# The first norm of a decoder layer on Trainium2: three blocks ahead, then two groups of three

## The chip, the cores and the metric

One core of a Trainium2 chip runs the whole kernel. The metric is the device time of one execution in microseconds. The engines are TensorE (PE, with its weight loads as PEld), VectorE (DVE), ScalarE (ACT), GpSimd (POOL) and SyncE (SP). Each of PE, DVE, ACT and POOL works through its own list of instructions in order; SP only issues transfers.

## What is computed

One step of a hybrid decoder layer for 1024 prompt tokens and 32 sample tokens (8 sequences of 4), model width 1024. Cut to what matters here:

```
h = rmsnorm(x, norm1)                       # x: 1056 tokens x 1024
z = h @ w_in                                # 6216 columns, split below
hq, hf, hi, hog, aq, ak, av, iq, ik, iw, ga, gb = split(z)
y_a = (rmsnorm(hgrn2(hq, hf, hi)) * silu(hog)) @ w_a     # gated recurrence, 4 heads
y_b = sparse_attention(aq, ak, av, iq, ik, iw) @ w_b     # top-256 keys of an indexer, 4 heads
x = x + (sigmoid(ga) * y_a + sigmoid(gb) * y_b) @ w_o
x = x + square(relu(rmsnorm(x, norm2) @ w_up)) @ w_down
y = rmsnorm(x, norm_f)
```

with `rmsnorm(x, g) = x * rsqrt(mean(x * x) + eps) * g`. The sample tokens also attend to 256 cached tokens of their sequence, whose pages are gathered.

## The kernel before

**First norm.** The 1056 tokens are nine blocks: 0 to 7 of 128 tokens, block 8 of 32. For each block: load `xt`; on ACT a Square with a running sum into `ssx`; `rstd_of` (lines 183 to 193) makes the reciprocal root `rsx` of it, with a variance step on DVE, a Sqrt on ACT, a Reciprocal and three short refinement steps on DVE; one DVE multiply writes the normed `ht` (L234); eight PE transposes turn it into a PSUM tile `hTp` (L238); ACT copies that to `hh`, rounded to fp32r (L239), and DVE takes the rest, `hl = hTp - hh` (L240). The blocks go through in `GROUPS`: 0, 1 and 2 singly, then (3, 4), (5, 6), (7, 8), and a group shares one `rsx`.

**Products.** Each product of `h` with a weight is made of three fp32r products: high by high, low by high, high by low (`gemm3`, lines 152 to 158). A weight tile is loaded into `wr` (one buffer), ACT casts its high part (L148) and DVE subtracts for its low part (L149), in `wload`, both at high priority. The first two weights are `whi` and `whog` of head 0; they are called in the loop when block 2 has been squared. The tokens are cut into three chunks of 352 columns, so chunk 0 needs blocks 0 to 2, chunk 1 blocks 2 to 5. `proj_two` runs chunk by chunk over the two weights, with 24 PE instructions for each weight and chunk.

**PSUM.** Eight banks: two of tag `g` (accumulators of the projections), two of tag `t` (single banks) and two pairs of tag `s`. `hTp` takes a pair of tag `s`, so a block's transposes wait until the copies of the block two before it have been made.

**Behind it.** The raw `xt` blocks are transposed too (`xTp`, L253, with an identity `idr` that is made from the last group's `rsx`), copied by ACT and stored by POOL for the residual. Then come, head by head, the recurrence, then the indexer and its top-k by bisection on DVE and ACT, with the gate projections `wgt` as work for PE beside it, then attention: scores `S`, DVE mask and maximum, ACT exponential (L896), PE transposes `pTp`, copies `pT` by ACT or DVE (L888), products `po`. For the sample group gathered value pages `vpg` are cast by ACT (`vsh`, L970) and split by DVE (`vsl`, L971). Merge, output projection and MLP follow.

**What sets the order.** The program is written in the order of the text, but a list scheduler with a timing model of its own places the instructions on each engine by their dependences and priorities. A change in one place can therefore set other places in another order.

Of the kernel before, what the change touches and what calls it, by code (L numbers as in the profile page):

```python
# [10 lines left out]
F32 = mybir.dt.float32  # L11
# [3 lines left out]
AF = mybir.ActivationFunctionType  # L15
ALU = mybir.AluOpType
# [3 lines left out]
D = 1024  # L20
# [15 lines left out]
N_UNITS = 26  # L36
DOTS_S, DOTS_L = "sstts", "sstsstss"
CUTS = (0, 352, 704, 1056)

GROUPS, FIRST_W = ((0,), (1,), (2,), (3, 4), (5, 6), (7, 8)), 2  # L40

TH, TC = 528, 264
ORDER = ("P1", "P2", "P6", "P5", "P7", "P4", "P3")
# [18 lines left out]
C_HQ, C_HF, C_HI, C_HOG, C_AQ, C_AK, C_AV, C_IQ, C_IK, C_GA, C_GB = (  # L62
    0, 512, 1024, 1536, 2048, 2560, 3072, 3584, 4096, 4168, 5192)
# [37 lines left out]
def hybrid_step(ctx: ExitStack, tc, x_prompt, x_sample, cache_k, cache_v, cache_idx_k, state_hgrn,  # L101
# [3 lines left out]
    nc = tc.nc  # L105
    dbg = dbg or {}

    cst = ctx.enter_context(tc.tile_pool(name="cst", bufs=1))
# [10 lines left out]
    def ps_t(name):  # L119
        return psum.tile([128, 512], F32, name=name, tag="t", bufs=2)  # L120

    def ps_s(name):
        return psum.tile([128, 2, 512], F32, name=name, tag="s", bufs=2)
# [5 lines left out]
    ident = cst.tile([128, 128], F32, name="ident")  # L129
# [8 lines left out]
    hh = big.tile([128, 8, T], F32R, name="hh", tag="hh")  # L138
    hl = big.tile([128, 8, T], F32R, name="hl", tag="hl")


    def wload(rows, c0, nk, m, name):
        raw = wp.tile([128, nk, m], F32, name=name + "r", tag="wr", bufs=1)
        nc.sync.dma_start(raw, rows[:, c0:c0 + m].rearrange("(k p) m -> p k m", p=128))
        wh = wp.tile([128, nk, m], F32R, name=name + "h", tag="wh", bufs=2)
        wl = wp.tile([128, nk, m], F32R, name=name + "l", tag="wl", bufs=2)
        with tc.high_priority():
            nc.scalar.copy(wh, raw)  # L148
            nc.vector.tensor_tensor(wl, raw, wh.bitcast(F32), op=ALU.subtract)  # L149
        return wh, wl  # L150

# [31 lines left out]
    def rstd_of(ss, n, scale, name):  # L183
        rt = sm.tile([128, 3, 9], F32, name=name, tag="rs", bufs=2)
        v, r, t = (rt[:ss.shape[0], a, :n] for a in range(3))
        nc.vector.tensor_scalar(v, ss, scale, EPS, op0=ALU.mult, op1=ALU.add)
        nc.scalar.activation(r, v, AF.Sqrt)
        nc.vector.reciprocal(r, r)

        nc.vector.scalar_tensor_tensor(t, r, -0.5, r, op0=ALU.mult, op1=ALU.mult)  # L190
        nc.vector.tensor_tensor(t, t, v, op=ALU.mult)
        nc.vector.scalar_tensor_tensor(r, t, 1.5, r, op0=ALU.add, op1=ALU.mult)
        return r
# [7 lines left out]
    g1 = U.get([128, 1024], F32, "g1")  # L201
    nc.scalar.dma_start(g1, bass.AP(tensor=norm1.tensor, offset=norm1.offset, ap=[[0, 128], [1, D]]))

    def tok(tb):
        n = 128 if tb < 8 else NS
        return n, slice(tb * 128, tb * 128 + n)
# [3 lines left out]
    nc.scalar.activation(zc, ones[:, 0:1], AF.Sqrt)  # L210
    hr = Ring(U, 6)
    xts = []
    first_w = None
    for grp in GROUPS:
        ss = sm.tile([128, 3], F32, name="ssx", tag="ssx", bufs=3)
        if 8 in grp:
            nc.vector.memset(ss, 1.0)
        hts = []
        for a, tb in enumerate(grp):
            n, cs = tok(tb)  # L220
            xt = U.get([128, 1024], F32, "xt")
            src = x_prompt[0, cs, :] if tb < 8 else x_sample.rearrange("s q d -> (s q) d")
            nc.sync.dma_start(xt[:n], src)
            ht = hr.get([128, 1024], F32, "ht")
            nc.scalar.activation(ht[:n], xt[:n], AF.Square, accum_out=ss[:n, a:a + 1])
            xts.append(xt)
            hts.append(ht)
        if not first_w and grp[-1] >= FIRST_W:
            first_w = [wload(w_in[0], C_HI, 8, 128, "whi"), wload(w_in[0], C_HOG, 8, 128, "whog")]
        rs = rstd_of(ss[:, :len(grp)], len(grp), 1.0 / D, "rsx")  # L230
        for a, tb in enumerate(grp):
            n, cs = tok(tb)
            ht = hts[a]
            nc.vector.scalar_tensor_tensor(ht[:n], xts[tb][:n], rs[:n, a:a + 1], g1[:n], op0=ALU.mult, op1=ALU.mult)  # L234
            pst = ps_s("hTp")
            pv = pst.rearrange("p a (b c) -> p (a b) c", c=128)
            for k in range(8):
                nc.tensor.transpose(pv[:, k, :n], ht[:n, k * 128:(k + 1) * 128], ident[:n, :n])  # L238
            nc.scalar.copy(hh[:, :, cs], pv[:, :, :n])  # L239
            nc.vector.tensor_tensor(hl[:, :, cs], pv[:, :, :n], hh[:, :, cs].bitcast(F32), op=ALU.subtract)  # L240
    U.put(g1)
    hr.close()

# [3 lines left out]
    for tb in range(NTB):  # L247
        n, cs = tok(tb)
        xT = U.get([128, 8, 128], F32, "xT")
        for k0 in (0, 4):  # L250
            pst = ps_t("xTp")
# [141 lines left out]
    for h in range(4):  # L393
        vT = U.get([128, T], F32, "vT")

        def ev_og(ps, sl, c):
            sg_ = sm.tile([128, CH], F32, name="sgo", tag="c352", bufs=2)
            sg_ = sg_[:, :sl.stop - sl.start]
            nc.scalar.activation(sg_, ps, AF.Sigmoid)
            nc.vector.tensor_tensor(sil[:, sl], ps, sg_, op=ALU.mult)  # L400

        def ev_i(ps, sl, c):
# [29 lines left out]
        b = U.get([128, T], F32, "b")  # L432
# [33 lines left out]
        for c in range(1, 8):  # L466
            e = eb[:, c * 128 + 127:c * 128 + 128]
            nc.vector.scalar_tensor_tensor(S[:, c, :], S[:, c - 1, :], e, puv[:, c, :],
                                           op0=ALU.mult, op1=ALU.add)
# [14 lines left out]
        for s in range(8):  # L484
            e = eb[:, NP + 4 * s + 3:NP + 4 * s + 4]
            nc.vector.scalar_tensor_tensor(sn[:, s, :], s0[:, s, :], e, pu2[:, s, :],
                                           op0=ALU.mult, op1=ALU.add)
# [13 lines left out]
        for li, B in enumerate(LEVELS):  # L501
            n = T if B <= 2 else NP
# [22 lines left out]
            ps = ps_t("lev")  # L525
# [699 lines left out]
    raw = {}  # L1225
# [335 lines left out]
```

## Time and profile before

| | us |
|---|---|
| three runs | 1783.34, 1787.66, 1788.07 |
| their median | 1787.66 |
| the profiled execution | 1783.03 |
| its span, first to last instruction | 1781.3 |
| PE busy | 1713.2 (96% of the span) |
| DVE busy | 1229.4 (69%) |
| ACT busy | 877.3 (49%) |

The busy time of PE is the sum of its instructions' rows; where a row's end is modelled it overlaps the next one's start. A row of a timeline gives the start in us from the first instruction, the length, the engine, the line, the operation, what it writes and reads, and how often it is repeated in the row; in brackets stands how long the engine was idle before it and what ended that. The granted clock is the share of TensorE's full speed.

### The profile page before, as it was taken

How to read it: one execution, taken by the hardware profiler on the slowest of the kernel's cores; microseconds unless marked ns; L12 is line 12 of the kernel's file. 1: busy time of each engine (PE TensorE's matmuls, PEld its weight loads, DVE VectorE, ACT ScalarE, POOL GpSimd, SP SyncE). 2: the span in 40 equal slices, each digit the busy share in tenths (PEclk: the TensorE clock that was granted, in tenths of full speed). 3: DMA queues.
4: the chain of work that ended last, by engine and by line, in shares of the span. 5: the costliest groups of instructions: out<-in, count | busy, mean ns of one | idle time of the engine just before them, and what ended most of it. 6: DMA issues, size and time to landing. Idle time of an engine off the chain costs nothing. (4 is left out here: it accounts for less than half of the span.)

```text
span 1781.3 us, 31007 instructions
## 1 busy us (share of the span) xinstructions
PE 1713.2 (96%) x11980; PEld 1650.2 (93%) x11980; DVE 1229.4 (69%) x2776; ACT 877.3 (49%) x1645; POOL 231.9 (13%) x296
## 2 busy tenths in 40 slices
PE   6999999999999999988999999999999999999997
PEld 6999999998999998886899998999999999999987
DVE  7275584745799997974747568867777676666565
ACT  6456465334578843224733445444444555454432
POOL 1100000013000014650200231000000011111100
PEclk9999999999999999999999999999999999999999
DMA  5411111231223233461543341544444857686752
GB/s 168 134 50 49 50 56 49 62 93 37 69 77 96 75 109 114 156 190 58 160 150 109 109 133 51 199 138 145 139 143 140 287 133 213 161 222 157 202 155 98
DMA packets 162132, 219.77 MB, mean 123 GB/s; under 512 B 12032, under 2 KB 117792, under 8 KB 161984
## 3 DMA queue, kind: packets, MB, share of 16 engines
q1 hardware_dynamic: 138048, 150.76, 26.6%
q0 software_dynamic: 16880, 57.85, 12.5%
q10 hardware_dynamic: 7056, 9.18, 1.5%
q8 instruction: 94, 1.54, 0.4%
q14 instruction: 54, 0.44, 0.1%
HBM read 140.31 MB, written 74.60 MB: 121 GB/s over the span
## 5 line engine op out<-in xcount | busy, mean ns | idle before, releaser
L1336 PE MATMUL pua<-h2P,wP 128*128 128x264 f32 x1248 | 198.8, 285 | 1.1 <-ACT uu L1405 0.9
L1336 PEld LDWEIGHTS pua<-h2P,wP 128*128 128x128 f32 x1248 | 170.7, 188 | 2.0 <-ACT uu L1405 1.7
L1336 PE MATMUL pua<-h2a,wP 128*128 128x264 f32 x960 | 161.2, 287 | 6.4 <-ACT uu L1405 3.2
L1405 ACT COPY uu<-pua 128x264 f32<-128x264 f32 x192 | 72.4, 378 | 174.9 <-PE pua L1336 162.8
L1336 PEld LDWEIGHTS pua<-h2a,wP 128*128 128x128 f32 x960 | 134.2, 188 | 11.1 <-ACT uu L1405 5.8
L156 PE MATMUL wgt<-hh,wgth 128*128 128x352 f32 x384 | 126.1, 328 | 0.0
L158 PE MATMUL wgt<-hh,wgtl 128*128 128x352 f32 x384 | 125.3, 326 | 0.0
L157 PE MATMUL wgt<-hl,wgth 128*128 128x352 f32 x384 | 124.6, 325 | 0.0
L1336 PE MATMUL pua<-h2b,wP 128*128 128x264 f32 x672 | 119.9, 285 | 1.0 <-ACT uu L1405 0.9
L1336 PE MATMUL puc<-h2P,wP 128*128 128x264 f32 x720 | 113.8, 285 | 0.0
L1336 PEld LDWEIGHTS pua<-h2b,wP 128*128 128x128 f32 x672 | 97.3, 188 | 1.8 <-ACT uu L1405 1.4
L1336 PEld LDWEIGHTS puc<-h2P,wP 128*128 128x128 f32 x720 | 98.1, 188 | 0.4 <-DVE h2P L1353 0.2
L777 ACT ACTIVATE jkA<-sc,bstg 128x1024 bf16<-128x1024 bf16 (+5 forms) x93 | 87.1, 936 | 21.3 <-DVE bstg L796 6.0
L1303 DVE TENSOR_TENSOR wP<-w1r,wP 128x512 fp32r<-128x512 f32 (+2 forms) x96 | 62.7, 654 | 33.5 <-ACT wP L1302 33.0
L772 DVE TENSOR_SCALAR_CACHE_REDUCE jkD<-sc,bstg 128x768 bf16<-128x768 f32 (+3 forms) x96 | 84.4, 879 | 0.9
L1302 ACT CAST wP<-w1r 128x512 fp32r<-128x512 f32 (+2 forms) x96 | 56.9, 593 | 45.5 <-PE puc L1336 22.1
L1336 PE MATMUL puc<-h2a,wP 128*128 128x264 f32 x384 | 72.7, 288 | 2.9 <-ACT h2a L1352 0.9
L156 PEld LDWEIGHTS wgt<-hh,wgth 128*128 128x128 f32 x384 | 72.2, 188 | 2.0 <-issue 1.0
L157 PEld LDWEIGHTS wgt<-hl,wgth 128*128 128x128 f32 x384 | 72.3, 188 | 1.1 <-issue 0.5
L158 PEld LDWEIGHTS wgt<-hh,wgtl 128*128 128x128 f32 x384 | 72.1, 188 | 1.2 <-issue 0.6
L1392 POOL TENSOR_SCALAR one<-uu 128x1 f32<-128x1 f32 x30 | 7.7, 257 | 492.5 <-ACT uu L1405 492.5
L1409 DVE TENSOR_TENSOR hd<-puc,uu 128x264 f32<-128x264 f32 x64 | 27.6, 431 | 56.7 <-ACT uu L1405 55.9
(792 smaller groups left out, 5143.2 us busy)
## 6 DMA issues: line engine op xcount, KB each, us to landing
hc_d<-hd SPq DMA_DIRECT2D x56, 264.0 KB, 2.6
x_d<-hd POOLq DMA_DIRECT2D x28, 528.0 KB
h2P<-hc_d SPq DMA_DIRECT2D x45, 264.0 KB, 5.1
sg_d<-gst ACTq DMA_DIRECT2D x48, 176.0 KB, 2.2
h2a<-hc_d SPq DMA_DIRECT2D x32, 264.0 KB, 5.5
wgtr<-in_w_in_dram SPq DMA_DIRECT2D x16, 512.0 KB, 4.1
qb<-q_d POOLq DMA_DIRECT2D x16, 512.0 KB
w1r<-in_w_up_dram SPq DMA_DIRECT2D x16, 512.0 KB, 4.1
```

The costliest lines, as they stand in the source:

```text
L156: nc.tensor.matmul(ps, wh, xh, start=(k == 0), stop=False)
L157: nc.tensor.matmul(ps, wh, xl, start=False, stop=False)
L158: nc.tensor.matmul(ps, wl, xh, start=False, stop=(k == n - 1))
L772: nc.vector.tensor_scalar(jkD[:, 0, :L], SC[i], s if isinstance(s, float) else s[:, a:a + 1], 0.0, op0=op, op1=ALU.add, accum_out=out[:, a ...
L777: nc.scalar.activation(jkA[:, 0, :(i + 1) * 128], src(i), AF.Sign, bias=thr[:, a:a + 1], accum_out=cnt[:, a:a + 1])
L1302: nc.scalar.copy(w[:, 0, :n], src)
L1303: nc.vector.tensor_tensor(w[:, 1, :n], src, w[:, 0, :n].bitcast(F32), op=ALU.subtract)
L1336: nc.tensor.matmul(ps, w[:, a, k], x[:, b, sl], start=(q in "P1P2P5" and k == n_ == 0), stop=(k == k1 - k0 - 1 and n_ == 2), skip_group_ch ...
L1392: eng.tensor_scalar(one, src, 1.0, 1.0, op0=ALU.max, op1=ALU.min)
L1405: nc.scalar.copy(uu[c][:, {"P1": u1, "P6": 1, "P7": 2}[q]], ps)
L1409: nc.vector.tensor_tensor(hd[j][1][:, s2], bank(j, "P5", c), uu[c][:, 2], op=ALU.add)
```

## The change

Blocks 0, 1 and 2 go through the norm up to their multiply before any of them is transposed and split (`norm`, `turn`). Block 2 is transposed into two single banks of tag `t` (`hTq`), four transposes each, and copied in halves. Blocks 3 to 8 go in two groups of three. The weights of head 0 are cast at plain priority; `whi` comes behind block 0. Four tiny DVE instructions make constants that depend on a result: `one` (1.0, from the third norm) is the scale of the first copies and of the cast of `whi`, so that they follow it; `inv` (1/1024, from `hh` of a group's first block) is the factor in the next group's variance; `onel` (1.0, from the last norm) is the scale of the first sigmoid.

```
--- before.py
+++ after.py
@@ -37,8 +37,6 @@
 DOTS_S, DOTS_L = "sstts", "sstsstss"
 CUTS = (0, 352, 704, 1056)
 
-GROUPS, FIRST_W = ((0,), (1,), (2,), (3, 4), (5, 6), (7, 8)), 2
-
 TH, TC = 528, 264
 ORDER = ("P1", "P2", "P6", "P5", "P7", "P4", "P3")
 
@@ -139,13 +137,13 @@
     hl = big.tile([128, 8, T], F32R, name="hl", tag="hl")
 
 
-    def wload(rows, c0, nk, m, name):
+    def wload(rows, c0, nk, m, name, late=None):
         raw = wp.tile([128, nk, m], F32, name=name + "r", tag="wr", bufs=1)
         nc.sync.dma_start(raw, rows[:, c0:c0 + m].rearrange("(k p) m -> p k m", p=128))
         wh = wp.tile([128, nk, m], F32R, name=name + "h", tag="wh", bufs=2)
         wl = wp.tile([128, nk, m], F32R, name=name + "l", tag="wl", bufs=2)
-        with tc.high_priority():
-            nc.scalar.copy(wh, raw)
+        with tc.high_priority() if late is None else ExitStack():
+            nc.scalar.activation(wh, raw, AF.Copy, scale=1.0 if late is None else late)
             nc.vector.tensor_tensor(wl, raw, wh.bitcast(F32), op=ALU.subtract)
         return wh, wl
 
@@ -210,8 +208,9 @@
     nc.scalar.activation(zc, ones[:, 0:1], AF.Sqrt)
     hr = Ring(U, 6)
     xts = []
-    first_w = None
-    for grp in GROUPS:
+
+    def norm(grp, inv=1.0 / D):
+
         ss = sm.tile([128, 3], F32, name="ssx", tag="ssx", bufs=3)
         if 8 in grp:
             nc.vector.memset(ss, 1.0)
@@ -225,19 +224,54 @@
             nc.scalar.activation(ht[:n], xt[:n], AF.Square, accum_out=ss[:n, a:a + 1])
             xts.append(xt)
             hts.append(ht)
-        if not first_w and grp[-1] >= FIRST_W:
-            first_w = [wload(w_in[0], C_HI, 8, 128, "whi"), wload(w_in[0], C_HOG, 8, 128, "whog")]
-        rs = rstd_of(ss[:, :len(grp)], len(grp), 1.0 / D, "rsx")
+        rs = rstd_of(ss[:, :len(grp)], len(grp), inv, "rsx")
         for a, tb in enumerate(grp):
             n, cs = tok(tb)
-            ht = hts[a]
-            nc.vector.scalar_tensor_tensor(ht[:n], xts[tb][:n], rs[:n, a:a + 1], g1[:n], op0=ALU.mult, op1=ALU.mult)
-            pst = ps_s("hTp")
-            pv = pst.rearrange("p a (b c) -> p (a b) c", c=128)
-            for k in range(8):
-                nc.tensor.transpose(pv[:, k, :n], ht[:n, k * 128:(k + 1) * 128], ident[:n, :n])
-            nc.scalar.copy(hh[:, :, cs], pv[:, :, :n])
-            nc.vector.tensor_tensor(hl[:, :, cs], pv[:, :, :n], hh[:, :, cs].bitcast(F32), op=ALU.subtract)
+            nc.vector.scalar_tensor_tensor(hts[a][:n], xts[tb][:n], rs[:n, a:a + 1], g1[:n], op0=ALU.mult,
+                                           op1=ALU.mult)
+        return grp, hts, rs
+
+    def turn(grp, hts, rs):
+
+        for ht, tb in zip(hts, grp):
+            n, cs = tok(tb)
+            if tb == 2:
+
+                pvs = [(k0, ps_t("hTq").rearrange("p (b c) -> p b c", c=128)) for k0 in (0, 4)]
+            else:
+                pvs = [(0, ps_s("hTp").rearrange("p a (b c) -> p (a b) c", c=128))]
+            for k0, pv in pvs:
+                nk = 8 // len(pvs)
+                for k in range(nk):
+                    nc.tensor.transpose(pv[:, k, :n], ht[:n, (k0 + k) * 128:(k0 + k + 1) * 128], ident[:n, :n])
+            for k0, pv in pvs:
+                ks = slice(k0, k0 + 8 // len(pvs))
+                nc.scalar.activation(hh[:, ks, cs], pv[:, :, :n], AF.Copy, scale=one[:, 0:1] if tb < 2 else 1.0)
+                nc.vector.tensor_tensor(hl[:, ks, cs], pv[:, :, :n], hh[:, ks, cs].bitcast(F32), op=ALU.subtract)
+
+
+    normed = [norm((tb,)) for tb in range(3)]
+
+    one = cst.tile([128, 1], F32, name="one")
+    nc.vector.tensor_scalar(one, normed[2][2][:, 0:1], 1.0, 1.0, op0=ALU.max, op1=ALU.min)
+    turn(*normed[0])
+    first_w = [wload(w_in[0], C_HI, 8, 128, "whi", late=one)]
+    turn(*normed[1])
+    turn(*normed[2])
+    inv = 1.0 / D
+    for grp in ((3, 4, 5), (6, 7, 8)):
+        normed = norm(grp, inv)
+        if len(first_w) == 1:
+            first_w.append(wload(w_in[0], C_HOG, 8, 128, "whog", late=1.0))
+        turn(*normed)
+
+        inv = cst.tile([128, 1], F32, name=f"inv{grp[0]}")
+        nc.vector.tensor_scalar(inv, hh[:, 7, tok(grp[0])[1]][:, 127:128].bitcast(F32), 1.0 / D, 1.0 / D,
+                                op0=ALU.max, op1=ALU.min)
+    rs = normed[2]
+
+    onel = cst.tile([128, 1], F32, name="onel")
+    nc.vector.tensor_scalar(onel, rs[:, 0:1], 1.0, 1.0, op0=ALU.max, op1=ALU.min)
     U.put(g1)
     hr.close()
 
@@ -396,7 +430,7 @@
         def ev_og(ps, sl, c):
             sg_ = sm.tile([128, CH], F32, name="sgo", tag="c352", bufs=2)
             sg_ = sg_[:, :sl.stop - sl.start]
-            nc.scalar.activation(sg_, ps, AF.Sigmoid)
+            nc.scalar.activation(sg_, ps, AF.Sigmoid, scale=onel if h == c == 0 else 1.0)
             nc.vector.tensor_tensor(sil[:, sl], ps, sg_, op=ALU.mult)
 
         def ev_i(ps, sl, c):
```

On ACT at the start, from the square root of the second norm (`rsx`; `ht,ssx` is a square, `whih` and `whogh` are the weights' casts), before:

```order
L187 ACTIVATE rsx<-rsx 128x1
L225 ACTIVATE ht,ssx<-xt 128x1024
L239 CAST hh<-hTp 128x8x128
L148 CAST whih<-whir 128x1024
L187 ACTIVATE rsx<-rsx 128x1
L225 ACTIVATE ht,ssx<-xt 128x1024
L239 CAST hh<-hTp 128x8x128
L225 ACTIVATE ht,ssx<-xt 128x1024 x3
L187 ACTIVATE rsx<-rsx 128x2 x2
L225 ACTIVATE ht,ssx<-xt 128x1024
L239 CAST hh<-hTp 128x8x128
L225 ACTIVATE ht,ssx<-xt 32x1024
```

and now:

```order
L185 ACTIVATE rsx<-rsx 128x1
L224 ACTIVATE ht,ssx<-xt 128x1024
L185 ACTIVATE rsx<-rsx 128x1
L224 ACTIVATE ht,ssx<-xt 128x1024 x2
L249 ACTIVATE hh<-hTp,one 128x8x128
L146 ACTIVATE whih<-whir,one 128x1024
L249 ACTIVATE hh<-hTp,one 128x8x128
L224 ACTIVATE ht,ssx<-xt 128x1024
L249 ACTIVATE hh<-hTq 128x4x128 x2
L224 ACTIVATE ht,ssx<-xt 128x1024 x2
L224 ACTIVATE ht,ssx<-xt 32x1024
L185 ACTIVATE rsx<-rsx 128x3
```

The third norm's root has moved ahead of the first copies, two squares stand before the first `hh`, and three squares before the root that blocks 3 to 5 share.

On DVE, from the weight difference `whogl` to the last group's multiplies (`ht`; `rsx` is a root's steps), before:

```order
L149 TENSOR_TENSOR whogl<-whogr,whogh 128x1024
L240 TENSOR_TENSOR hl<-hTp,hh 128x8x128
L188 RECIPROCAL rsx<-rsx 128x2
L240 TENSOR_TENSOR hl<-hTp,hh 128x8x128
L190 SCALAR_TENSOR_TENSOR rsx<-rsx 128x2
L191 TENSOR_TENSOR rsx<-rsx 128x2
L192 SCALAR_TENSOR_TENSOR rsx<-rsx 128x2
L234 SCALAR_TENSOR_TENSOR ht<-xt,rsx,g_88 128x1024
L234 SCALAR_TENSOR_TENSOR ht<-xt,rsx,g_88 32x1024
```

and now:

```order
L147 TENSOR_TENSOR whogl<-whogr,whogh 128x1024
L230 SCALAR_TENSOR_TENSOR ht<-xt,rsx,g_88 128x1024 x3
L250 TENSOR_TENSOR hl<-hTp,hh 128x8x128
L269 TENSOR_SCALAR inv_237<-hh 128x1
L250 TENSOR_TENSOR hl<-hTp,hh 128x8x128
L184 TENSOR_SCALAR rsx<-ssx,inv_237 128x3
L250 TENSOR_TENSOR hl<-hTp,hh 128x8x128
L186 RECIPROCAL rsx<-rsx 128x3
L188 SCALAR_TENSOR_TENSOR rsx<-rsx 128x3
L189 TENSOR_TENSOR rsx<-rsx 128x3
L190 SCALAR_TENSOR_TENSOR rsx<-rsx 128x3
L230 SCALAR_TENSOR_TENSOR ht<-xt,rsx,g_88 128x1024 x2
```

The last group's reciprocal stood between two `hl`; now the multiplies of blocks 3 to 5 come first, then their three `hl`, and the reciprocal of blocks 6 to 8 behind these.

On PE at the same place, the end of chunk 0 of `whog` up to chunk 1 of `whi`, before:

```order
L157 MATMUL whog<-hl,whogh 128x352
L158 MATMUL whog<-hh,whogl 128x352
L253 MATMUL xTp<-idr,xt 128x128 x8
L238 MATMUL hTp<-ident,ht 128x128 x8
L253 MATMUL xTp<-idr,xt 128x128 x4
L156 MATMUL whi<-hh,whih 128x352
L157 MATMUL whi<-hl,whih 128x352
L158 MATMUL whi<-hh,whil 128x352
```

and now:

```order
L246 MATMUL hTp<-ident,ht 128x128 x16
L156 MATMUL whog<-hh,whogl 128x352
L154 MATMUL whog<-hh,whogh 128x352
L155 MATMUL whog<-hl,whogh 128x352
L156 MATMUL whog<-hh,whogl 128x352
L154 MATMUL whog<-hh,whogh 128x352
L155 MATMUL whog<-hl,whogh 128x352
L156 MATMUL whog<-hh,whogl 128x352
L246 MATMUL hTp<-ident,ht 128x128 x24
L287 MATMUL xTp<-idr,xt 128x128 x8
L246 MATMUL hTp<-ident,ht 128x32 x8
L287 MATMUL xTp<-idr,xt 128x128 x4
```

Before, the transposes of blocks 3 to 7 are spread over chunk 0, the last eight of them standing among `xTp`; now those of blocks 3 and 4 stand behind 17 products of `whog` (with all 24 of `whi` ahead of them) and those of 5, 6 and 7 in one row behind its end, with block 8 before chunk 1.

On ACT in the attention stage, from the last copy `pT` ahead of the first `vsh` to the second, before (`gst` is a gate's copy, `s__` with a number an exponential):

```order
L888 COPY pT<-pTp 128x512
L896 ACTIVATE s__7451,mx<-s__7451,mx 128x256
L970 CAST vsh<-vpg 128x1024
L357 COPY gst<-wgt 128x352
L358 DMA sg_d<-gst 128x352
L148 CAST wgth<-wgtr 128x1024
L357 COPY gst<-wgt 128x352
L358 DMA sg_d<-gst 128x352
L896 ACTIVATE s__7469,mx<-s__7469,mx 128x384
L970 CAST vsh<-vpg 128x1024
L357 COPY gst<-wgt 128x352
L888 COPY pT<-pTp 128x128
```

and now:

```order
L922 COPY pT<-pTp 128x512
L1004 CAST vsh<-vpg 128x1024
L930 ACTIVATE s__7454,mx<-s__7454,mx 128x256
L391 COPY gst<-wgt 128x352
L392 DMA sg_d<-gst 128x352
L930 ACTIVATE s__7472,mx<-s__7472,mx 128x384
L922 COPY pT<-pTp 128x128
L922 COPY pT<-pTp 128x256
L930 ACTIVATE s__7492,mx<-s__7492,mx 128x512
L922 COPY pT<-pTp 128x384
L1004 CAST vsh<-vpg 128x1024
L930 ACTIVATE s__7515,mx<-s__7515,mx 128x640
```

The second `vsh` has moved from ahead of the 128-wide `pT` to behind the 384-wide one.

## Rows read from the trace of the kernel before

**Rows 1.** Waits of PE, whole run: us in total, times, longest us.

```profile
PE hTp L238 <- DVE rsx L186: 14.5, 3, 9.8
...
PE po L891 <- ACT pT L888: 9.0, 6, 6.0
```

**Rows 2.** Windows of 50 us: window, length, busy us (and instructions) of each engine.

```profile
50.00:100.00 50.00, 50.00 (x331) 49.40 (x330) 21.20 (x28) 26.59 (x41) 5.30 (x6) 1.00 0.37 107
```

**Rows 3.** Timeline of PE at the start.

```profile
21.33 1.94 PE L238 MATMUL hTp<-ident,ht 128*128 128x128 f32 x8 [1.03 <-DVE ht L234]
...
22.92 0.64 PE L156 MATMUL whi<-hh,whih 128*128 128x352 f32 x1
...
25.76 0.32 PE L158 MATMUL whi<-hh,whil 128*128 128x352 f32 x1
...
25.92 0.32 PE L156 MATMUL whi<-hh,whih 128*128 128x352 f32 x1
...
35.56 1.04 PE L238 MATMUL hTp<-ident,ht 128*128 128x128 f32 x8
...
36.79 0.40 PE L156 MATMUL whi<-hh,whih 128*128 128x352 f32 x1
...
39.20 0.68 PE L238 MATMUL hTp<-ident,ht 32*128 32x32 f32 x8
```

**Rows 4.** Timeline of ACT at the start.

```profile
11.77 1.01 ACT L239 CAST hh<-hTp 128x1024 fp32r<-128x1024 f32 x1 [0.79 <-PE hTp L238]
...
12.68 1.05 ACT L148 CAST whih<-whir 128x1024 fp32r<-128x1024 f32 x1
...
16.71 1.05 ACT L225 ACTIVATE ht<-xt 128x1024 f32<-128x1024 f32 x1
```

**Rows 5.** Timeline of DVE at the start.

```profile
11.96 0.15 DVE L186 TENSOR_SCALAR rsx<-ssx 128x1 f32<-128x1 f32 x1
...
15.09 0.15 DVE L188 RECIPROCAL rsx<-rsx 128x1 f32<-128x1 f32 x1
...
15.27 0.16 DVE L190 SCALAR_TENSOR_TENSOR rsx<-rsx 128x1 f32<-128x1 f32 x1
...
16.94 1.28 DVE L234 SCALAR_TENSOR_TENSOR ht<-xt,rsx,g 128x1024 f32<-128x1024 f32 x1
...
27.09 1.22 DVE L240 TENSOR_TENSOR hl<-hTp,hh 128x1024 fp32r<-128x1024 f32 x1
...
32.56 0.29 DVE L246 TENSOR_SCALAR idr<-ident,zc 128x128 f32<-128x128 f32 x1
...
34.17 0.79 DVE L311 TENSOR_SCALAR scr<-scr 128x64 int32<-128x64 int32 x7
```

**Rows 6.** Loads of block 4 (issue; landing after it) and of `whog`.

```profile
5.94 0.62 SPq L223 DMA_DIRECT2D xt<-in_x_prompt_dram  x1
...
xt<-in_x_prompt_dram SPq DMA_DIRECT2D x1, 512.0 KB, 7.9
...
whogr<-in_w_in_dram SPq DMA_DIRECT2D x1, 512.0 KB, 5.5
```

**Rows 7.** A window behind the wait at 800 (PEclk third from the end), and slow products.

```profile
804.00:811.00 7.00, 4.32 (x14) 3.15 (x15) 3.90 (x11) 3.75 (x8) 1.98 (x2) 0.52 0.30 90
...
150.18 0.49 PE L156 MATMUL whf<-hh,whfh 128*128 128x352 f32 x1
...
150.47 0.49 PE L157 MATMUL whf<-hl,whfh 128*128 128x352 f32 x1
```

**Rows 8.** Timelines of PE and ACT around 806 us.

```profile
806.22 0.79 PE L891 MATMUL po<-pT,vt 128*128 128x128 f32 x2 [6.00 <-ACT pT L888]
...
804.60 1.04 ACT L970 CAST vsh<-vpg 128x1024 fp32r<-128x1024 f32 x1 [6.66 <-DMA vpg<-in_cache_v_dram,ids]
...
805.89 0.27 ACT L888 COPY pT<-pTp 128x128 f32<-128x128 f32 x1
...
809.80 0.48 ACT L888 COPY pT<-pTp 128x384 f32<-128x384 f32 x1 [0.76 <-PE pTp L885]
```

## The prediction

> **What bounds the kernel now.** First read the list of waits of TensorE (PE) over the whole run: 14.5 us stand before `hTp`, the transposes of the first norm, and 9.0 us before `po` in the attention stage, 6.0 of them in one piece [rows 1]. Then the windows: from 50 to 100 us PE is busy all the time [rows 2]. What the change does at the start therefore reaches the end whole, unless a later stage has slack to swallow it. So the start is followed instruction by instruction in the timelines of PE, ScalarE (ACT) and VectorE (DVE) [rows 3 to 5], and compared at one mark: the first product of chunk 1 of `whi`, at 36.79 us before [rows 3]. By then PE has done `hTp` of blocks 0 to 7, twelve `xTp`, and chunk 0 of `whi` and `whog`. In the changed order block 8 is turned ahead of that mark too, which takes 0.68 us before [rows 3]; so the mark to beat is 37.47.
>
> **The change, step by step.** The clock times below come from walking the changed rows with the durations of before: on ACT a square 1.05 us, a full copy 0.91 to the next start [rows 4], half copies 0.5, an estimate, since they read half as much; on DVE a difference `hl` or `wl` 1.22, a multiply 1.28, each of the four short steps from reciprocal to multiply 0.18 to 0.2 [rows 5].
>
> *Third norm, earlier.* The variance of block 2 is ready at 11.96 + 0.15 [rows 5]. Its square root follows at once, at 12.15, where it stood behind two copies that run until 13.6 [rows 4]. Reciprocal 12.4, multiply 13.15 to 14.45, against 16.94 before [rows 5]; its transposes into the two extra banks take 1.94 us [rows 3], to 16.4.
>
> *First copies, later.* The squares of blocks 3 and 4 now stand ahead of the first `hh`. Block 4 lands at 5.94 + 7.9 = 13.84 [rows 6], so its square starts at 13.85 and `hh` of block 0 at 14.9, where it ran at 11.77 [rows 4]. `whih` 15.8, `hh` of block 1 16.7, the square of block 5 17.6, the half copies 18.7 and 19.2. DVE follows: `hl` of block 0 15.9, `whil` 17.1, `hl` of block 1 18.3, the first half of `hl` of block 2 done at 20.3. Dense work on `whi` chunk 0 begins at 20.4, against 22.92 for its first product [rows 3]. That is the change's gain, some 2.5 us, as long as PE can go on.
>
> *Second group, later.* Blocks 3 to 5 share one square root, which stands behind the squares of 6, 7 and 8 (19.7, 20.75, 21.8): 22.85. `whogh` 22.95, `whogl` 24.0 to 25.2. The load of `whog` is issued when `whil` is done, 18.3, and lands 5.5 later by its old duration [rows 6], at 23.8; that would move these two by 0.85, which is hidden, since PE comes to them later still. Multiplies from 25.2, the last ready at 29.1.
>
> *What PE then does.* It has 24 products of `whi` and 17 of `whog` in its queue ahead of the first transpose of block 3. A product starts 0.16 us after the last one from 25.76 on [rows 3]; at half clock, later in the run, 0.29 [rows 7]. Taking the slow one until 25.65, where before's turned quick, 18 are done by then and 23 more take 3.7 us: block 3 starts at 29.35. Bounds: if all run quickly, the last 15 wait for `whogl` at 25.2 and end at 27.7; if none does, 32.5.
>
> *The chain behind it.* Eight quick transposes take 1.04 us [rows 3]. Block 3 is turned at 30.4, its `hh` done 31.4, its `hl` 32.65: only now is its bank free for block 5, 32.7 to 33.75. `hh` of 5 34.8, `hl` of 5 36.0. In DVE's order the reciprocal of blocks 6 to 8 stands behind this `hl`; four short steps and the multiply end at 38.05. PE, which has nothing ready between, stands from 33.7 to 38.1: 4.4 us. Block 6 to 39.15; block 7 behind its own multiply to 40.45. `idr` stands behind the last multiply (40.6) and seven short operations of 0.11 (seven took 0.79) and takes 0.29 [rows 5]: 41.65, another 1.2 us of waiting, then eight `xTp` to 42.75. Block 8 needs the bank of block 6, whose `hl` stands behind `idr` and seven more short ones, 42.45 to 43.65: 1 us again. Block 8 to 44.35, four `xTp`, and the mark at 44.85. Each row overlaps the next by 0.05 to 0.1 us, so over this chain the sum is some 0.4 too long: 44.45.
>
> Sum of the start: 44.45 - 37.47 = **+7.0 us**; with the bounds of block 3's start, +5.3 to +10.1.
>
> *Edits at nothing.* `one`, `inv` and `onel` are four DVE instructions on one column, of the 0.15 us of the variance row [rows 5], counted where they stand in the chain. Copies that scale, in place of plain ones: the trace has none of this form; between nothing and 0.1 us for each of ten, most of it under waits; I take none. SyncE issues its loads in the same order; `whog` alone comes later, above, and the two loads behind it are not wanted before chunk 2. GpSimd's `xT_d` stores follow `xT` by the same shift, and nobody waits for them. From about 75 to 480 us the orders of all engines are as before, so the shift goes through.
>
> *The attention stage.* From the top-k to about 830 us the scheduler also sets another order; behind it the order is as before. The one place that rows price is the 6.00 us wait [rows 8]: the second `vsh` cast, waiting for its gather until 804.60, stands ahead of the `pT` copy that `po` needs. Now it stands behind the 384-wide `pT`. From the start of the 128-wide one to the end of that it was 809.80 + 0.48 - 805.89 = 4.4 us [rows 8]. But the 39 gate products (6.2 us at 0.16) that stood between the last `po` and the first transpose of this head are now spent earlier, so the gather, issued when `vsl` is done, comes that much later against PE. Bounds: 6.0 gained, where the gather has landed when the cast is reached; 6.2 - 4.4 = 1.8 lost, where the cast holds the next exponential instead. The rest of the permuted rows I price at nothing, between 3 us lost and gained, half of that one wait. I take 0 for the stage, nearer to the loss, because PE's filler is worth its own time wherever it stands.
>
> So 1783.03 + 7.0 + 0 = 1790.0 against the profiled execution. That one lies with the fastest of the three runs (1783.34), 4.6 below their median of 1787.66; against the median it is 1787.66 + 7.0 = **1794.7**.
>
> **A clock that falls in the new waits.** In the wait that ended at 806.22 [rows 8] the granted clock fell: it is 0.52 from 804 to 811, the lower of its two levels of 1.2 and 2.4 GHz [rows 7]. The wait of 4.4 us from 33.7 is shorter, but transposes with two more waits follow it. If the clock falls there, blocks 6 and 7 take 1.94 each, the eight `xTp` as much, block 8 and four more some 2.2: the mark comes 1.5 later, and the start costs +8.5. The Trainium skill, "TensorE: Matmul & The Clock Gate", Part 1, says that the clock drops to 1.2 GHz when the engine idles and comes back after sustained matmul work. By that rule the fall is to be expected, and the sum would be +8.5 and not +7.0; the wait at 800 agrees with it.
>
> **Rivals.**
> 1. *Forecast*: the start loses 7.0, the stage gives nothing: 1794.7. For it: every step is an in-order queue whose rows are known. 0.52.
> 2. *The clock falls in the waits of 33 to 44 us*, or chunk 0 runs slowly to its end: 1787.66 + 8.5 to 10.1 = 1796 to 1798. For it the fall after 800; against it the shorter wait. 0.14.
> 3. *Not slower, because the wait at 800 goes*: the gather lands before the cast is reached. That takes 6.0 us and the low clock behind it, about 1.5: 1787.66 + 7.0 - 6.0 to 7.5 = 1787 to 1789. It decides as soon as the gather lands within 4.4 us of the first `pT`. Against it the moved gate products. 0.26, of which 0.03 with further gains there, below the line.
> 4. *The early start holds*: PE does not stand at block 6 and keeps its 2.5 us: 1785. It would need `hl` of block 5 to be no longer ahead of the reciprocal, which the order denies, or a far quicker copy. 0.08, of which 0.03 with the gain of rival 3.
>
> **How the numbers follow.** A measurement of this kernel can tell about 0.3%, 5.4 us, from no change: the line on the slow side is 1793. Of the forecast 0.36 lie above it and 0.16 below (the start near its lower bound, or some gain in the stage). Slower: 0.36 + 0.14 = 0.50. Same: 0.16 + 0.23 + 0.05 = 0.44. Faster: 0.03 + 0.03 = 0.06. The range runs from rival 4 at 1785, which takes in rival 3, to 1801: the upper bound of the start, 10.1, with the stage's 3 lost.
>
> **What would show it.** After: dense `whi` from about 20 us, block 3 turned near 29, a PE wait of 3 to 5 us before block 6 that ends with its multiply on DVE, two of about 1 us behind it, chunk 1 of `whi` at 43 to 46; from there to 480 us the same work 6 to 9 us later. In the attention stage either the wait of `po` on `pT` is down from 9.0 to about 3, or a wait of several us stands a few blocks later. The forecast is wrong if chunk 1 starts before 41, or if PE's waiting from 650 to 900 us differs by more than 4 us from before.

## The result and the profile after

The changed kernel takes 1799.21 us (median of 15 runs, 1792.39 to 1805.33) beside 1787.06 us of the kernel before (15 runs): ratio 1.0065, 95% interval 1.005 to 1.008, so 9 to 14 us slower, 11.6 by the ratio. Beside the experiments on another chip it came out at 1.0076 (1.005 to 1.0101). The forecast, 1794.7, had the sign and stands in its range, but the loss is larger than its 7.0: of its two terms the start came out at 7.0 and 8.4 us in two profiled executions, and the attention stage, taken at nothing, costs 5 to 7 us.

From the page of the changed kernel: its span, PE's busy time and PE's clock in 40 slices.

```profile
span 1798.4 us, 31000 instructions
...
PE 1723.3 (96%) x11980; PEld 1658.5 (92%) x11980; DVE 1228.6 (68%) x2776; ACT 879.7 (49%) x1645; POOL 231.4 (13%) x296
...
PEclk8999999899999999999999999999999999999999
```

The waits of PE over the whole run (us in total, times, longest), as in [rows 1]:

```profile
PE S L904 <- DVE mx L908: 5.9, 4, 3.5
PE po L925 <- DVE pT L922: 5.4, 3, 3.7
...
PE hTp L246 <- DVE ht L230: 4.8, 2, 4.5
PE whi L154 <- ACT hh L249: 4.8, 1, 4.8
PE po L925 <- ACT pT L922: 3.3, 6, 0.9
```

The 9.0 us of `po` behind ACT's `pT` are down to 3.3, as rival 3 wanted; two waits of 3.5 and 3.7 us, for DVE, stand in their place. At the start 4.8 us stand before `whi` and 4.5 before block 6.

The start on PE, as in [rows 3]:

```profile
14.50 1.09 PE L246 MATMUL hTq<-ident,ht 128*128 128x128 f32 x8 [0.80 <-DVE ht L230]
20.35 0.66 PE L154 MATMUL whi<-hh,whih 128*128 128x352 f32 x1 [4.76 <-ACT hh L249]
...
30.17 1.91 PE L246 MATMUL hTp<-ident,ht 128*128 128x128 f32 x16
...
39.13 3.65 PE L246 MATMUL hTp<-ident,ht 128*128 128x128 f32 x16 [4.46 <-DVE ht L230]
...
45.85 0.41 PE L154 MATMUL whi<-hh,whih 128*128 128x352 f32 x1
```

One row of ACT's timeline, the square of block 3:

```profile
13.36 1.06 ACT L224 ACTIVATE ht<-xt 128x1024 f32<-128x1024 f32 x1 [1.01 <-DMA xt<-in_x_prompt_dram]
```

Two windows (busy us of PE, weight loads, DVE, ACT and GpSimd; the granted clock is third from the end):

```profile
37.10:43.90 6.80, 4.77 (x23) 4.80 (x24) 6.69 (x22) 2.76 (x4) 1.13 (x2) 0.50 0.00 0
...
50.00:100.00 50.00, 50.00 (x334) 49.18 (x333) 13.89 (x23) 24.23 (x39) 7.97 (x9) 1.00 0.43 130
```

The mark, the first product of chunk 1 of `whi`, is at 45.85, 8.4 behind 37.47; from 50 to 100 us PE has no slack, as in [rows 2]. The row of ACT tells where a part of the 8.4 is from: the square of block 3 waits 1.01 us for its load. In the other profiled execution of the same kernel (e9 below) that square found its load there. Its ACT:

```profile
12.16 0.20 ACT L185 ACTIVATE rsx<-rsx 128x1 f32<-128x1 f32 x1 [1.15 <-DVE rsx L184]
12.49 1.06 ACT L224 ACTIVATE ht<-xt 128x1024 f32<-128x1024 f32 x1
...
14.78 1.10 ACT L249 ACTIVATE hh<-hTp,one 128x1024 fp32r<-128x1024 f32 x1
```

and its PE:

```profile
19.49 0.66 PE L154 MATMUL whi<-hh,whih 128*128 128x352 f32 x1 [3.01 <-ACT hh L249]
...
28.81 1.91 PE L246 MATMUL hTp<-ident,ht 128*128 128x128 f32 x16
...
37.78 3.65 PE L246 MATMUL hTp<-ident,ht 128*128 128x128 f32 x16 [4.46 <-DVE ht L230]
...
44.50 0.41 PE L154 MATMUL whi<-hh,whih 128*128 128x352 f32 x1
```

and a window of it:

```profile
35.10:41.90 6.80, 4.12 (x20) 4.15 (x21) 6.66 (x24) 2.13 (x2) 0.60 (x2) 0.50 0.00 0
```

Here the mark is 7.0 late, 1.35 earlier than in the first execution. Of that, 0.86 stands at the first product of `whi` (19.49 against 20.35) and goes with the load. The other 0.5 stands in chunk 0, where 16 products ran at the lower clock here (starts 0.29 apart) and 20 in the first execution. The chain that the forecast walked stands on DVE in the first execution: the difference of block 5, then the reciprocal of blocks 6 to 8, the short steps, the multiplies.

```profile
35.76 1.23 DVE L250 TENSOR_TENSOR hl<-hTp,hh 128x1024 fp32r<-128x1024 f32 x1 [0.91 <-ACT hh L249]
36.90 0.17 DVE L186 RECIPROCAL rsx<-rsx 128x3 f32<-128x3 f32 x1
...
37.70 2.48 DVE L230 SCALAR_TENSOR_TENSOR ht<-xt,rsx,g 128x1024 f32<-128x1024 f32 x2
```

**The attention stage.** Two executions of one kernel can lie 12 us apart by 480 us (last section), so spans don't tell what a stage costs. A window that begins and ends at the same products does: from 600 us of before to 845, 1380 products. Of the kernel before:

```profile
600.00:845.00 245.00, 225.09 (x1380) 202.69 (x1379) 191.89 (x462) 95.42 (x194) 85.17 (x65) 0.99 0.39 121
```

of the changed kernel:

```profile
612.30:862.00 249.70, 228.27 (x1380) 205.37 (x1379) 192.52 (x480) 100.96 (x203) 85.06 (x65) 0.97 0.38 118
```

and of its other execution:

```profile
608.30:860.00 251.70, 231.14 (x1380) 207.38 (x1379) 192.51 (x480) 100.80 (x203) 85.13 (x65) 0.96 0.38 117
```

The stage is 4.7 and 6.7 us longer in the changed kernel. PE's idle time is nearly the same: 245.0 - 225.1 = 19.9 before, 21.4 and 20.6 after. What grew is the busy time of the same 1380 products, by 3.2 and 6.0 us, and the granted clock fell from 0.99 to 0.97 and 0.96. Two long waits stand in it. PE's timeline of the changed kernel, with the short wait ahead of the first:

```profile
679.35 0.71 PE L925 MATMUL po<-pT,vt 128*128 128x128 f32 x4 [0.46 <-ACT pT L922]
683.52 2.50 PE L904 MATMUL S<-kT,qT 128*128 128x512 f32 x4 [3.46 <-DVE mx L908]
...
818.37 1.77 PE L925 MATMUL po<-pT,vt 128*128 128x128 f32 x8 [3.68 <-DVE pT L922]
```

DVE's at the first of them, and the window behind it:

```profile
681.48 0.25 DVE L873 TENSOR_SCALAR pm<-jkD 128x384 bf16<-128x384 bf16 x1
...
682.90 0.56 DVE L908 CUSTOM_DVE_ANT_0 s__6497<-S,pm 128x384 f32<-128x384 f32 x1
```

```profile
682.20:689.00 6.80, 5.13 (x13) 3.80 (x14) 6.80 (x16) 1.51 (x4) 0.00 (x0) 0.50 0.00 0
```

The two other windows of the stage at the lower clock, the first of them behind the second wait:

```profile
818.70:822.10 3.40, 3.15 (x12) 1.86 (x11) 1.21 (x6) 0.61 (x2) 2.49 (x4) 0.50 0.50 152
839.20:842.60 3.40, 3.40 (x17) 3.06 (x16) 1.11 (x3) 2.52 (x4) 0.00 (x0) 0.50 0.00 0
```

The scores `S` of a row block wait until DVE has read an earlier block's scores out, which needs the mask `pm` of the top-k selection. In the kernel before, `pm` was written at 665.03 and the same `S` stood at 667.08, with other products of PE ahead of it and no wait (DVE's row, then PE's):

```profile
665.03 0.26 DVE L839 TENSOR_SCALAR pm<-jkD 128x384 bf16<-128x384 bf16 x1
...
667.08 1.35 PE L870 MATMUL S<-kT,qT 128*128 128x512 f32 x4
```

Counted from the start of its window, PE was ready for this `S` at nearly the same place (67.1 us before, 67.8 in the changed kernel), but DVE wrote `pm` at 65.0 before and at 69.2 now: in the new order it is DVE that comes later.

In the kernel before, the clock fell within the one wait of 6.0 us [rows 8] and stayed at the lower level for 6.8 us by the trace's clock records, from 803.9 to 810.7 [rows 7]. In the changed kernel 13.7 us of the stage are at that level: 6.8 from within the wait of 3.5, 3.4 behind the wait of 3.7, and 3.4 at 839.2, where no wait ahead is longer than 0.8. In the other execution it is 20.5: 6.8 and 13.7, at two waits of 3.4. The Trainium skill, "TensorE: Matmul & The Clock Gate", section "HAM oscillation — how this bites in real kernels", prices such a time at half of itself; the trace agrees: 13.7 - 6.8 = 6.9, half 3.4, where busy time grew 3.2, and 20.5 - 6.8 = 13.7, half 6.9, where it grew 6.0.

### The profile page after: what moved, and what is told of

It is laid out like the page before. It is cut to its first block, busy times and chain, and to the rows that moved or that the text cites. A ratio compares the mean times of both kernels' runs of the same rounds, so it can differ in the third digit from the quotient of the medians.

```text
span 1798.4 us, 31000 instructions
## 1 busy us (share of the span) xinstructions
PE 1723.3 (96%) x11980; PEld 1658.5 (92%) x11980; DVE 1228.6 (68%) x2776; ACT 879.7 (49%) x1645; POOL 231.4 (13%) x296
```

## The experiments

Ratio and interval are against the kernel before on the same chip; its medians were 1790.9 (e1 to e4), 1782.7 (e5 to e8) and 1781.3 (e9 to e12). "Start" is the delay of the mark (against 37.47, or 36.79 where block 8 still stands behind it, as before); for e4 and e11 it is that of the mark and the time of the added transposes behind it. "Stage" is the length of the 1380 products less 245.0. Both are from the one profiled execution; the time in us is worked out from the ratio.

| | start | stage | sum | ratio (interval) | us |
|---|---|---|---|---|---|
| changed kernel | +8.4 | +4.7 | 13.1 | 1.0065 (1.0050 to 1.0080) | +11.6 |
| e9, the same again | +7.0 | +6.7 | 13.7 | 1.0076 (1.0050 to 1.0101) | +13.5 |
| e10, stage order back | +7.4 | 0.0 | 7.4 | 1.0023 (1.0005 to 1.0042) | +4.1 |
| e2, block 5 banks | +6.7 | +0.7 | 7.4 | 1.0027 (1.0009 to 1.0046) | +4.8 |
| e3, free root | +4.7 | +5.3 | 10.0 | 1.0048 (1.0029 to 1.0066) | +8.6 |
| e5, both | +3.2 | 0.0 | 3.2 | 1.0009 (0.9995 to 1.0022) | +1.6 |
| e6, norms only | +1.8 | +0.3 | 2.1 | 1.0024 (1.0010 to 1.0038) | +4.3 |
| e7, filled wait | +8.5 | -0.6 | 7.9 | 1.0032 (1.0019 to 1.0045) | +5.7 |
| e8, banks only | +2.1 | -0.2 | 1.9 | 0.9986 (0.9970 to 1.0002) | -2.5 |
| e12, as e8 | +1.7 | +0.4 | 2.1 | 1.0008 (0.9990 to 1.0025) | +1.4 |
| e4, shift | +4.3 | +1.2 | 5.5 | 1.0003 (0.9984 to 1.0023) | +0.5 |
| e11, stage order alone | +1.1 | +3.8 | 4.9 | 1.0015 (0.9998 to 1.0031) | +2.7 |
| e1, control | +0.5 | -0.5 | 0.0 | 0.9999 (0.9975 to 1.0022) | -0.2 |

**e1, control.** No edit.

> The kernel before, unchanged, run as if it were a change: its ratio to itself should be 1.000 within 0.002. It gives the granted clock of its single runs, which the comparison of the change lacks. Theory A (the start costs some 8 us, and the permuted attention stage the other 4 of the 12 us between the medians): its mean granted clock lies where the changed kernel's does in its quicker runs, 0.987 to 0.991. Theory B (the start costs some 8, and the other 4 are stretches at the lower clock, which come more often with the changed kernel): it stays at 0.990 to 0.993 in nearly all runs, where the changed kernel shows 0.983 to 0.991.

Its mean granted clocks are 0.985 to 0.992 in 12 runs, so theory B's "0.990 to 0.993 in nearly all" fell, and A's words on the clock fit. What the lower clock has to do with the stage came out only with the window of equal products.

**e2, block 5 banks.**

```
-            if tb == 2:
+            if tb in (2, 5):
```

> The changed kernel with block 5 also transposed into two single banks of its own. The start stays as it is but for 0.4 us (block 5 need not wait for the bank of block 3), and the scheduler's order of the attention stage falls back to that of the kernel before. Mark (first product of chunk 1 of whi) at 45 to 46 by both theories. Theory A (the permuted attention stage costs 4 us): 1787 + 8 = 1795, and from 660 to 830 us the delay against before stays at that of the mark. Theory B (the order of that stage is worth nothing, the rest is low clock, met anywhere): 1797 to 1800, as the changed kernel.

The mark at 44.21 is 0.8 ahead of what both theories expected, 45 to 46 (they started from 45.85, the execution with the late load). The stage, +0.7, is as theory A says; the time, +4.8, is below its +8, which the interval just holds. B's +10 and more is outside.

**e3, free root.**

```
-    inv = 1.0 / D
...
-        normed = norm(grp, inv)
+        normed = norm(grp)
...
-        inv = cst.tile([128, 1], F32, name=f"inv{grp[0]}")
-        nc.vector.tensor_scalar(inv, hh[:, 7, tok(grp[0])[1]][:, 127:128].bitcast(F32), 1.0 / D, 1.0 / D,
-                                op0=ALU.max, op1=ALU.min)
```

> The changed kernel with 1/D a constant, so that the square root of blocks 6 to 8 need not wait for hh of block 3. On DVE the multiplies of 6 to 8 then stand right behind those of 3 to 5, ahead of the three hl, not behind them. If the 4.5 us wait before block 6 comes from the root and the reciprocal standing behind hh and hl of blocks 3 to 5, as the prediction's chain has it: that wait goes, block 5 waits for hl of block 3 instead (about 1.5 to 2 us more), idr is there by 36, the mark comes at 40 to 42, and the time is 1787 + 3 to 5 = 1790 to 1792 if the attention stage, whose order is a third one here, gives nothing. If the groups of three are the cause by themselves (one chain of three multiplies, two banks for three blocks), the wait only moves: mark at 44 to 46, 1795 to 1799.

The start's chain is confirmed (rows of DVE, then of PE): the multiplies of 6 to 8 follow those of 3 to 5, ahead of the three `hl`; block 5 now waits 2.63 us for the bank of block 3, and block 6, turned right behind it, no longer 4.46 for its own multiply; the mark is at 41.48, in the range of the first theory. The time is not (+8.6): the stage, which stands in a third order here, is 5.3 longer as well.

```profile
26.38 3.67 DVE L230 SCALAR_TENSOR_TENSOR ht<-xt,rsx,g 128x1024 f32<-128x1024 f32 x3
...
30.76 3.67 DVE L230 SCALAR_TENSOR_TENSOR ht<-xt,rsx,g 128x1024 f32<-128x1024 f32 x3
```

```profile
35.74 3.10 PE L246 MATMUL hTp<-ident,ht 128*128 128x128 f32 x16 [2.63 <-DVE hl L250]
...
41.48 0.41 PE L154 MATMUL whi<-hh,whih 128*128 128x352 f32 x1
```

**e4, shift.** In the kernel before, ahead of the transposes of block 8:

```
+            for k in range(56 if tb == 8 else 0):
+                nc.tensor.transpose(pv[:, k % 8, :n], ht[:n, (k % 8) * 128:(k % 8 + 1) * 128], ident[:n, :n])
```

> The kernel before, with 56 more transposes of 0.13 us into the bank of block 8 ahead of its own: 7.3 us of work on PE at the start and no new wait; every engine's order is otherwise that of before but for four chunk-boundary swaps. If a delay at the start reaches the end whole and nothing else comes with it: 1787 + 6.5 to 7.3 = 1793.5 to 1794.5, and the granted clock as in the control. If a mere shift of the later stages brings low-clock stretches or new waits of its own: 1798 to 1800. If a later stage swallows it: under 1791.

The edit was smaller than meant: block 8 has 32 rows, a transpose of it takes 0.066 us, and the 56 took 3.67. Of that +0.5 (-2.9 to +4.1) was found: it neither shows nor excludes that 3.7 us reach the end whole.

**e5, both.** The edits of e2 and e3 together.

> Both edits at once: the root of blocks 6 to 8 free (1/D a constant), and block 5 in two banks of its own; with the second the attention stage stands in the order of the kernel before again. If the permuted attention stage costs some 5 us (A), this is the free root's start (mark 41.5, 4.7 later than in the kernel before) with that stage's price gone: 4 to 5 us over the kernel before, about 1.0025, and from 640 to 850 us no delay is added. If the order of that stage is worth nothing and the excess is low clock met by chance (B): 1.0045 to 1.005, as with the free root alone.

Start +3.2, stage 0.0, time +1.6. The interval, -0.9 to +3.9, leaves out B's 1.0045 by far and A's +4 to 5 by little: A's stage is as expected, its start and its time came out smaller. It is 7 us less than e3, which differs by the banks of block 5 and the stage's order; start and stage of the two profiles differ by 1.5 and 5.3, together 6.8.

**e6, norms only.**

```
-    first_w = [wload(w_in[0], C_HI, 8, 128, "whi", late=one)]
+    first_w = [wload(w_in[0], C_HI, 8, 128, "whi")]
```

and the same for `whog`, plain scales for the first `hh`, and the free root of e3.

> The changed kernel without its bindings: the casts of whi and whog ranked first as before, the first copies hh not held behind the third norm, the last root free. What is left of the change is three norms written ahead, the two banks for block 3 of the tokens and the groups of three; the attention stage stands in the order of before. If the late start comes from the bindings (copies held behind the squares, the root held behind hh): the mark within 2 us of before's 36.8 and 0.999 to 1.0015. If groups of three cost by themselves (three multiplies in a row on DVE ahead of the first hl): the mark 3 to 5 later and 1.002 to 1.003. If the early norms bring their 2.5 us once nothing holds the rest: 0.9985 and the first dense product at 20 to 21.

The mark is at 39.25: 2.5 behind 36.8, past the 2 of the first theory and short of the 3 of the second, and 1.8 late when block 8, which is turned ahead of it here, is counted. The ratio is above the first theory's range and in that of the second. So the two can't be told apart here. The early gain of the third is excluded: the third norm falls behind the first cast again, and block 2 is transposed at 18.44, as before.

**e7, filled wait.** 28 more transposes, of the rows of block 5, ahead of those of block 6 (the lines that set `fill` are left out).

```
+            if tb in fill:
+                src, m = fill[tb]
+                for k in range(m):
+                    nc.tensor.transpose(pvs[0][1][:, k % 8, :n], src[:n, (k % 8) * 128:(k % 8 + 1) * 128], ident[:n, :n])
```

> The changed kernel with 28 more transposes (of the rows of block 5, into the bank of block 6, which block 6 then overwrites) in the wait of 4.5 us before block 6; 3.6 us of work at full clock, so the wait falls to about 1. The attention stage stands in the order of before. If the clock falls because of that wait (rival 2): the granted clock stays at its upper level from 37 to 44, blocks 6 and 7 take 2 us instead of 3.65, and from the first product of whi to the mark it is 24.0 us, where it was 25.5; the time 1.001 to 1.003. If the fall has another cause: 25.5 again.

PE's rows, then the window that was at 0.50:

```profile
33.76 3.28 PE L246 MATMUL hTp<-ident,ht 128*128 128x128 f32 x28
38.03 1.09 PE L250 MATMUL hTp<-ident,ht 128*128 128x128 f32 x8 [0.99 <-DVE ht L230]
...
43.27 0.65 PE L250 MATMUL hTp<-ident,ht 32*128 32x32 f32 x8 [2.89 <-DVE inv L278]
...
45.95 0.64 PE L154 MATMUL whi<-hh,whih 128*128 128x352 f32 x1
```

```profile
35.00:42.00 7.00, 4.19 (x35) 3.51 (x33) 6.86 (x20) 2.59 (x3) 1.13 (x2) 1.00 0.00 0
```

Filling the wait keeps the clock up from 35 to 42 us, as rival 2 says; but the mark does not move: 45.95 - 20.47 = 25.5 from the first product of `whi`, as in the changed kernel's first execution. Two differences cancel in that number: chunk 0 ran quicker here, 8.7 us up to block 3 against 9.8, and from block 3 to the mark it took 16.8 against 15.7 in both executions of the changed kernel. Blocks 6 and 7 are turned faster, block 8 then waits 2.89 us for DVE, and the clock falls behind that wait, at 44.8 by the clock records. The order near block 8 differs a little, so this shows that DVE can set the mark, not what the fall costs there.

**e8 and e12, banks only.** In the kernel before, block 2 in two banks, its copies in halves.

> The kernel before with one part of the change alone: block 2 transposed into two single banks, its copies in halves; nothing else, and the attention stage as before. No bank was waited for there in the kernel before (block 2 waited for its root), but blocks 3 and 4 need not wait for the first copies any more: between 1 us gained and nothing, 0.9990 to 1.0005. If the two banks were what delays the start: 1.002 or more.

> The two banks for block 2 alone once more, since its interval just reached 1: if they gain what the first runs showed, 0.9986 again and the two together clear of 1; if that was chance, 0.9995 to 1.001, as its mark 1.4 later than before's says.

-2.5 and +1.4: no difference that 24 runs can tell; the second lies in the range that was expected if the first was chance. The mark is 2.1 and 1.7 later than before. In 22 of the 24 runs the mean granted clock is 0.989 to 0.994, with a median of 0.992, where the kernel before has 0.989 beside them; why it lies higher is open. This is the version that comes nearest to beating both kernels; it beats the changed one.

**e9, the changed kernel again.**

> The changed kernel itself, beside the next two on the same chip: 1.005 to 1.008 of the kernel before, as it was.

1.0076, from 6 runs, in the range expected.

**e10, stage order back.** The changed kernel with 10 of the short transposes of e4, which is enough for the scheduler to set the stage as before.

> The changed kernel with 10 more transposes of 32 columns (0.066 us each, 0.7 in all) into the bank of block 8 ahead of its own: the start is that of the change and 0.7 later, but the scheduler now sets the order of the kernel before in the attention stage. If the order of that stage costs some 5 us: 1.004, that is 4 us less than the changed kernel beside it, and from 640 to 850 us no delay is added. If the order is worth nothing: 0.7 us more than the changed kernel.

The start is the changed one (+7.4). The stage is before's, in its idle time (19.7 us), its busy time and its clock:

```profile
606.10:851.10 245.00, 225.28 (x1380) 202.60 (x1379) 192.29 (x462) 95.44 (x194) 85.30 (x65) 0.99 0.38 121
```

The time is +4.1 where e9 beside it has +13.5; the intervals (0.9 to 7.5 and 8.9 to 18.0) don't meet. The sums of start and stage in the two profiles differ by 6.3 of these 9.4.

**e11, stage order alone.** The kernel before with 16 of them.

> The kernel before with 16 such transposes (1.1 us): the start of before and 1.1 later, but the attention stage in the order that the free root had, with the top-k selection of DVE ahead of a block's scores. If the order costs some 5 us by itself: 1.003 to 1.0035, and the trace shows a PE wait of 3 to 4 us for the scores' maximum near 675 us, with the granted clock at its lower level behind it, and 4.5 to 5.5 us added from 640 to 850. If the order is worth nothing: 1.0006.

The trace does what the first theory says: the wait for the scores' maximum, and a stage 3.8 longer at a lower clock.

```profile
673.35 1.98 PE L872 MATMUL S<-kT,qT 128*128 128x512 f32 x4 [3.38 <-DVE mx L876]
```

```profile
602.10:850.90 248.80, 227.36 (x1380) 205.69 (x1379) 194.72 (x480) 100.81 (x203) 83.87 (x65) 0.97 0.37 119
```

The time, +2.7 (-0.4 to 5.5), lies between the theories and excludes neither.

## Why the prediction was right, and where not

**The start, +7.0: right up to block 6, in part by luck behind it.** In the execution whose loads were in time the forecast's walk stands to within 0.6 us: the root of block 2 at 12.16 (forecast 12.15), block 3 turned at 28.81 (29.35), a wait of 4.46 (4.4), block 6 at 37.78 (38.1), the mark at 44.50 (44.45). Dense work began at 19.49, 0.9 earlier than forecast, with nothing of it left at the mark. Behind block 6 two errors cancel: the two waits of about 1 us that the walk has there are 0.3 and 0.6 in the trace, and the turning of blocks 6 and 7, 2.4 us in the walk, takes 3.65 at the lower clock. e3 and e5 show the cause that it named: with the last root free the start is 2.3 us shorter (e3 against e9) and 3.5 (e5 against e2).

**Missed: what a late load does.** The change puts the squares of blocks 3 and 4 ahead of every first copy. Where the load of block 3 was 1.01 us late, dense work began 0.86 later. The rest of the 1.35 between the two marks is the clock in chunk 0, of which the forecast had 18 slow products where 16 and 20 were found.

**Copies that scale, at nothing: 0.1 each.** `hh` took 1.09 to 1.10 us against 1.01 [rows 4]. The Trainium skill, "ScalarE: Activation LUTs", section "What ACT_TABLE_LOAD costs", gives 93 ns for each pointer operand; the trace agrees. The walk of the start came out right all the same.

**Rival 2, the clock in the waits of 33 to 44 us.** Its condition came true (0.50 in both executions) and its price, 1.5 on the mark, did not show: the mark of 44.50 has the fall in it and stands where the forecast put it without one. What the fall costs by itself is open, since e7, with the clock up there, met another wait and a later fall.

**The attention stage, 0: the step that was mis-sized.** The forecast balanced waits, and of waits it was right: the 6.0 us went, as rival 3 said, others came, and the idle time of PE is the same within 1.5 us, as its sign of at most 4 us asked. But in taking 0 for the stage it priced the moved waits at their length alone, though it had the clock in rivals 2 and 3. In this stage the clock fell at the waits of 3.5 and 3.7 us to the lower of the two levels of 1.2 and 2.4 GHz, as it did at the one of 6.0; one long wait had become two middling ones, with 13.7 and 20.5 us at the lower level in place of 6.8, and the stage 4.7 and 6.7 us longer. Its two bounds for the stage, +1.8 and +3, make 4.8 together: the first execution is at that, the second beyond it. Eight kernels in which PE and DVE have before's order there, instruction by instruction (e1, e2, e4 to e8, e10), lie within -0.6 and +1.2, and e12 at +0.4; the four executions with another order (the changed kernel twice, e3, e11) at +3.8 to +6.7. So it is shown that the order makes the stage longer, and by e10 that the time goes with it. That the clock falls because of the new waits is read from where the falls stand, and that the products that filled the gap at 667 were spent earlier is read from the traces; neither was tried by itself.

**"Reaches the end whole": open.** With the stage in before's order, the sum of start and stage is above the measured time in seven of the eight experiments that shift the start, by 0.7 to 5.0 us, and 2.2 below it in e6. So 2 to 3 us may be swallowed on the way, and one place for it stands in the traces. Between 420 and 441 us PE waits before `dots` and `wav`; in the kernel before:

```profile
PE dots L650 <- ACT r L656: 3.6, 2, 2.4
```

In the control it is 3.9 us. In nine of the twelve executions of other kernels it is at most 1.1, in the other three (e2, e3 and the changed kernel's first) 3.2 to 4.4. Why it goes in some and stays in others is not known. The sign "to 480 us the same work 6 to 9 us later" says little for the same reason: it was 8.4 in e9 and 12.5 in the first execution, but the kernel before is itself 12.2 later there in e1.

## What to carry to other kernels

A change at the start of a scheduled kernel can set another order 600 us later: compare the orders of the whole program, and price the far stage by a window of equal products. Count waits of TensorE by their number as well as by their length: here two of 3.5 and 3.7 us had more time at the lower clock with them than one of 6.0. A copy or a root that is bound to a later result to force an order moves everything queued behind it, on its own engine and on the next.

## What was not expected of the hardware

Single executions of one kernel differ by up to 1% (e1's 12 runs lie between 1780.5 and 1799.4 us), and in the pair that was profiled most of the difference is the granted clock. The same 2548 products, in the kernel before:

```profile
90.00:480.00 390.00, 384.68 (x2548) 369.10 (x2546) 243.60 (x419) 200.40 (x322) 37.73 (x49) 0.98 0.20 56
```

and in its control, e1:

```profile
90.50:492.20 401.70, 394.99 (x2548) 378.24 (x2546) 243.92 (x419) 200.70 (x322) 37.80 (x49) 0.96 0.19 54
```

Idle time is 5.3 and 6.7 us; busy time differs by 10.3. By the clock records 13.7 us of the first window and 34.1 of the second are at the lower level. The clock need not fall in a wait. Here are the same 16 products in either execution, with `whog` products right ahead of them and no wait, first of the kernel before, then of the control, where the fall stands at 258.8, among those `whog` products:

```profile
254.04 1.89 PE L533 MATMUL lev<-Qls,E 128*128 128x64 f32 x16
```

```profile
259.90 3.51 PE L533 MATMUL lev<-Qls,E 128*128 128x64 f32 x16
```

In which execution it falls at such a place was not predictable from the traces. The Trainium skill, "TensorE: Matmul & The Clock Gate", Part 1, says that the count of slow products at a kernel's start changes from run to run; here it does so at several places of the middle, and a single profile of each kernel would have put the change anywhere between 5 and 17 us.
